# Writing 128 KB of zeros through the store queue at the start of a row normalisation

## The chip, the core and the metric

The kernel runs on one core of a Trainium2 chip. A core has several engines that run their own instruction streams: VectorE (DVE in the profile), ScalarE (ACT), GpSimd (POOL), TensorE (PE, idle here) and SyncE (SP). Data move between the device's memory (HBM) and the on-chip memory (SBUF, 128 partitions) by DMA: an instruction on SP's or ACT's queue issues a transfer, and 16 DMA engines carry it out. The metric is device time in microseconds (us) of one execution, as the median of several runs. A profile is one further execution with a recorder on; its times belong to that execution.

## What is computed

Each row of 1024 numbers is divided by the sum of its absolute values.

```python
batch, seq, dim = 32, 512, 1024        # x: float32
def reference(x):
    sums = np.sum(np.abs(x), axis=-1, keepdims=True)
    return (x / (sums + 1e-8)).astype(np.float32)
```

That is 16,384 rows of 4 KB: 67.11 MB are read and 67.11 MB written.

## The kernel before

The rows are cut into 11 tiles. A tile holds `k` rows in each of the 128 partitions: `k` is 12 for the first ten tiles and 8 for the last (`rows`, L34). Tiles 0, 1 and the last (tile 10) come from the first 4096 rows of `x`, where a partition owns 32 neighbouring rows; tiles 2 to 9 are blocks of 1536 rows each (`piece`, L36). Tile 9 is the block that ends with the last row of the matrix, so the store of tile 9 is the one that writes the last 32 rows. In every tile a partition's rows are contiguous in HBM, so one DMA packet carries 48 KB (32 KB in the last tile), and a transfer has 128 such packets, eight on each DMA engine.

For each tile, in order:

- L88: SP issues the load into `x_tile`, one of four buffers (`BUFS`, L30). The first four loads need no buffer to come free. Load i+4 waits until the store of tile i has left the same buffer.
- L52 to L61: VectorE sums absolute values along the rows (`tensor_reduce`), adds the small constant and takes the reciprocal.
- L63, L70, L73: the rows are scaled in place, most of them by VectorE in one instruction with a broadcast factor (L63), a few one by one on VectorE (L70) or on ScalarE (L73), as `split` (L83) says for the first three and the last two tiles.
- L91: ACT issues the store of the tile.

The order is written out by hand (`manual_schedule`, L85): instructions stand on each engine in program order. SP's queue holds loads alone (the DMA queue q1), and ACT's queue holds stores alone (q10) among its scalings. Both queues are served by the same 16 DMA engines.

Of the kernel before, what the change touches and what calls it, by code (L numbers as in the profile page):

```python
# [1 line left out]

# [4 lines left out]

FP32 = mybir.dt.float32
EPS = 1e-8


@with_exitstack
def kernel(
    ctx: ExitStack,
    tc: tile.TileContext,
    x: bass.AP,
    out: bass.AP,
):
    nc = tc.nc
    P = nc.NUM_PARTITIONS  # L20

    x_flat = x.flatten_outer_dims()
    out_flat = out.flatten_outer_dims()
    n, d = x_flat.shape

    R = 12
    BUFS = 4  # L30
    HEAD = 32
    per_partition = n // P
    assert n % P == 0 and (per_partition - HEAD) % R == 0
    rows = [R] * ((per_partition - HEAD) // R + 2) + [HEAD - 2 * R]  # L34

    def piece(flat, i):  # L36
        head = flat[: P * HEAD, :].rearrange("(p r) d -> p r d", p=P)
        if i < 2:
            return head[:, R * i : R * (i + 1), :]
        if i == len(rows) - 1:  # L40
            return head[:, 2 * R :, :]
        a = P * (HEAD + R * (i - 2))
        return flat[a : a + P * R, :].rearrange("(p r) d -> p r d", p=P)

    sbuf = ctx.enter_context(tc.tile_pool(name="sbuf", bufs=BUFS))
    stats = ctx.enter_context(tc.tile_pool(name="stats", bufs=len(rows)))

    def normalize(x_tile, k, kv, kt):


        s = stats.tile([P, R], FP32)
        nc.vector.tensor_reduce(  # L52
            out=s[:, :k],
            in_=x_tile[:, :k, :],
            axis=mybir.AxisListType.X,
            op=mybir.AluOpType.add,
            apply_absolute_value=True,
        )
        nc.vector.tensor_scalar_add(out=s[:, :k], in0=s[:, :k], scalar1=EPS)  # L59
        inv = stats.tile([P, R], FP32)  # L60
        nc.vector.reciprocal(out=inv[:, :k], in_=s[:, :k])  # L61
        if kv:
            nc.vector.tensor_mul(  # L63
                out=x_tile[:, :kv, :],
                in0=x_tile[:, :kv, :],
                in1=inv[:, :kv].unsqueeze(2).to_broadcast([P, kv, d]),
            )
        for r in range(kv, kv + kt):
            row = x_tile[:, r, :]
            nc.vector.tensor_scalar_mul(out=row, in0=row, scalar1=inv[:, r : r + 1])  # L70
        for r in range(kv + kt, k):
            row = x_tile[:, r, :]
            nc.scalar.activation(  # L73
                out=row,
                in_=row,
                func=mybir.ActivationFunctionType.Copy,
                scale=inv[:, r : r + 1],
            )

    last = len(rows) - 1
    split = {0: (3, 4), 1: (0, 3), 2: (0, 3), last - 1: (0, 2), last: (5, 3)}  # L83

    with tc.manual_schedule():  # L85
        for i, k in enumerate(rows):
            x_tile = sbuf.tile([P, R, d], FP32)
            nc.sync.dma_start(out=x_tile[:, :k, :], in_=piece(x_flat, i))  # L88
            kt, ks = split.get(i, (0, 0))
            normalize(x_tile, k, k - kt - ks, kt)  # L90
            nc.scalar.dma_start(out=piece(out_flat, i), in_=x_tile[:, :k, :])  # L91


# [1 line left out]
_INS = ['x']  # L95
_OUTS = [((32, 512, 1024), 'float32')]


# [23 lines left out]
```

## Time and profile before

| | before |
|---|---|
| median of 3 runs | 317.42 us (317.39 to 317.75) |
| span of the profiled execution | 315.8 us |
| VectorE busy | 261.2 us, 83% of the span |
| ScalarE busy | 17.4 us, 6% |
| mean rate of the DMA engines | 425 GB/s over the span |
| loads: issue to landing, median of the ten of 6 MB | 38.0 us |
| stores: issue to landing, median of the ten of 6 MB | 47.4 us |
| first load issued / first tile's reduction begins | 0.73 / 17.65 us |
| first store issued | 38.67 us |
| last store issued | 294.08 us |

The span is the time from the first to the last instruction in the profile. The time of a run is somewhat larger, since it holds what lies around these instructions. Engines overlap, so busy shares do not add up; what counts is which wait ends last. The "chain of waits" follows the work back from the last instruction to whatever released it. A table of stretches gives, for windows of the span, how long each engine was busy and how much the DMA engines moved (a packet is counted where it starts). The packet records of the trace give start, length, size and queue of each DMA packet; the records of one DMA engine can be strung together, because each packet starts where the one before it ended.

### The profile page before, as it was taken

What the parts mean: (1) busy time and instruction counts of PE and PEld (TensorE: products, weight loads), DVE (VectorE), ACT (ScalarE), POOL (GpSimd) and SP (SyncE); (2) the same over time, 40 slices, a digit from 0 to 9 for tenths busy, and PEclk for the clock granted to TensorE, in tenths of its full rate; (3) what the DMA queues carried; (4) which work ended last, traced back from release to release, by engine and by line L of the source; (5) the groups of instructions that cost most, each with busy time, mean ns of one, the idle gap of its engine ahead of it and who ended that gap; (6) DMA issues with size and microseconds to landing.
All of it is one profiled execution on the core that took longest, in us unless ns stands there. A gap on an engine that the chain in (4) does not pass through costs nothing.

```text
span 315.8 us, 168 instructions
## 1 busy us (share of the span) xinstructions
DVE 261.2 (83%) x51; ACT 17.4 (6%) x16; POOL 0.2 (0%) x4
## 2 busy tenths in 40 slices
DVE  0079999999999999969996999799699969999200
ACT  0010404004000000000000000000000000201200
POOL 0000000000000000000000000000000000000000
DMA  8999999999999999999999999999999999999986
GB/s 324 473 398 448 448 361 430 405 486 405 405 486 405 405 486 411 423 467 405 448 436 411 479 405 411 473 417 405 473 417 411 467 413 450 421 442 423 473 374 282
DMA packets 3168, 134.22 MB, mean 425 GB/s; under 512 B 352, under 2 KB 352, under 8 KB 352
## 3 DMA queue, kind: packets, MB, share of 16 engines
q1 hardware_dynamic: 1584, 67.11, 49.8%
q10 hardware_dynamic: 1584, 67.11, 49.1%
HBM read 67.11 MB, written 67.11 MB: 425 GB/s over the span
## 4 chain that ended last, share of the span: by engine, by line
DVE 41%; DMA 33%; another core or an unknown queue 18%; issue 0%; SPq 0%; DVEq 0%
DVE s L52 23%; DMA x_tile<-in_x_dram 17%; DMA out_dram<-x_tile 16%; DVE x_tile L63 15%; DVE x_tile L70 1%; DVE inv L61 0%; DVE s L59 0%; SPq L88 0%; DVEq L117 0%
## 5 line engine op out<-in xcount | busy, mean ns | idle before, releaser
L52 DVE TENSOR_REDUCE s<-x_tile 128x12 f32<-128x12288 f32 (+1 forms) x11 | 138.2, 12561 | 31.5 <-DMA x_tile<-in_x_dram 31.5
L63 DVE TENSOR_TENSOR x_tile<-x_tile,inv 128x12288 f32<-128x12288 f32 (+3 forms) x10 | 113.6, 11358 | 0.5
L73 ACT ACTIVATE x_tile<-x_tile,inv 128x1024 f32<-128x1024 f32 x15 | 16.1, 1138 | 258.7 <-DVE inv L61 258.7
L70 DVE TENSOR_SCALAR x_tile<-x_tile,inv 128x1024 f32<-128x1024 f32 x8 | 5.5, 748 | 0.0
L61 DVE RECIPROCAL inv<-s 128x12 f32<-128x12 f32 (+1 forms) x11 | 2.5, 226 | 0.4
L73 ACT ACT_TABLE_LOAD x1 | 1.3, 1283 | 17.7 <-DMA x_tile<-in_x_dram 17.7
L59 DVE TENSOR_SCALAR s<-s 128x12 f32<-128x12 f32 (+1 forms) x11 | 1.9, 173 | 0.4
L106 POOL MEMSET const-bfloat16-1.0<- 128x1 bf16 x1 | 0.1, 102 | 0.0
L106 POOL MEMSET const-uint8-127<- 128x1 uint8 x1 | 0.1, 102 | 0.0
L106 POOL MEMSET const-float32-0.0<- 128x1 f32 x1 | 0.1, 99 | 0.2 <-issue 0.2
L106 POOL MEMSET const-float32-1.0<- 128x1 f32 x1 | 0.1, 99 | 0.0
## 6 DMA issues: line engine op xcount, KB each, us to landing
x_tile<-in_x_dram SPq DMA_DIRECT2D x10, 6144.0 KB, 38.0
out_dram<-x_tile ACTq DMA_DIRECT2D x10, 6144.0 KB, 47.4
x_tile<-in_x_dram SPq DMA_DIRECT2D x1, 4096.0 KB, 33.3
out_dram<-x_tile ACTq DMA_DIRECT2D x1, 4096.0 KB, 20.6
```

The costliest lines, as they stand in the source:

```text
L52: nc.vector.tensor_reduce(out=s[:, :k], in_=x_tile[:, :k, :], axis=mybir.AxisListType.X, op=mybir.AluOpType.add, apply_absolute_value=True,)
L59: nc.vector.tensor_scalar_add(out=s[:, :k], in0=s[:, :k], scalar1=EPS)
L61: nc.vector.reciprocal(out=inv[:, :k], in_=s[:, :k])
L63: nc.vector.tensor_mul(out=x_tile[:, :kv, :], in0=x_tile[:, :kv, :], in1=inv[:, :kv].unsqueeze(2).to_broadcast([P, kv, d]),)
L70: nc.vector.tensor_scalar_mul(out=row, in0=row, scalar1=inv[:, r : r + 1])
L73: nc.scalar.activation(out=row, in_=row, func=mybir.ActivationFunctionType.Copy, scale=inv[:, r : r + 1],)
L106: nc = _bacc.Bacc("TRN2", target_bir_lowering=False, num_devices=1)
```

## The change

Before the first load, VectorE fills a small tile of 16 partitions by 2 rows by 1024 floats with zeros, and ACT issues a store of it to the last 32 rows of the result: 128 KB in one contiguous piece, with 8 KB from each of the 16 partitions. The store of tile 9 later writes the same rows. The loop's body is split into three functions, and the first four loads stand ahead of the loop; the order of loads on SP, of stores on ACT and of the computation on VectorE is the same.

```diff
+    tiles = {}
+
+    def load(i):
+        x_tile = tiles[i] = sbuf.tile([P, R, d], FP32, name="x_tile")
+        nc.sync.dma_start(out=x_tile[:, : rows[i], :], in_=piece(x_flat, i))
+
+    def store(i):
+        nc.scalar.dma_start(out=piece(out_flat, i), in_=tiles[i][:, : rows[i], :])
+
+    def compute(i):
+        k = rows[i]
+        kt, ks = split.get(i, (0, 0))
+        normalize(tiles[i], k, k - kt - ks, kt)
+
     with tc.manual_schedule():
-        for i, k in enumerate(rows):
-            x_tile = sbuf.tile([P, R, d], FP32)
-            nc.sync.dma_start(out=x_tile[:, :k, :], in_=piece(x_flat, i))
-            kt, ks = split.get(i, (0, 0))
-            normalize(x_tile, k, k - kt - ks, kt)
-            nc.scalar.dma_start(out=piece(out_flat, i), in_=x_tile[:, :k, :])
+        zero = ctx.enter_context(tc.tile_pool(name="zero", bufs=1)).tile([16, 2, d], FP32, name="zero")
+        nc.vector.memset(zero, 0.0)
+        late = out_flat[n - 32 :, :].rearrange("(p r) d -> p r d", p=16)
+        nc.scalar.dma_start(out=late, in_=zero)
+        for i in range(BUFS):
+            load(i)
+        for i in range(len(rows)):
+            compute(i)
+            store(i)
+            if i + BUFS < len(rows):
+                load(i + BUFS)
```

## The prediction

> **What bounds the kernel now.** I read the table of DMA queues first, since the kernel only divides rows and moves every byte twice.
>
> ```profile
> ## 3 DMA queue, kind: packets, MB, share of 16 engines
> q1 hardware_dynamic: 1584, 67.11, 49.8%
> q10 hardware_dynamic: 1584, 67.11, 49.1%
> HBM read 67.11 MB, written 67.11 MB: 425 GB/s over the span
> ```
>
> q1 carries SP's loads, q10 ACT's stores. Their packets fill 98.9% of the 16 DMA engines' time: the transfers bound the kernel, and about 3.5 us of the span (1.1% of 315.8) is theirs to lose. Next, the chain of waits.
>
> ```profile
> 0.73 16.89 DMA x_tile<-in_x_dram
> 17.62 0.02 issue
> 17.65 12.96 DVE s L52
> ...
> 219.13 38.10 DMA x_tile<-in_x_dram
> 257.23 0.02 issue
> 257.25 12.96 DVE s L52
> ```
>
> VectorE waits 17.65 us for tile 0, and later some 2.5 to 2.9 us a tile for loads. It is not the bound at the end either: the last store is issued at 294.08 us, when, by the packet records, the engines still have some 9 us of the store before it to write (that one's last packets end at 303.3 to 304.7). So VectorE may be a few us late without an effect, and the end is set by how soon each DMA engine gets through its bytes. Third, the table of stretches: where do the engines fall short?
>
> ```profile
> core 0: us, DVE busy (x) ACT busy (x) POOL busy (x), PEclk, DMA share, GB/s
> 8.00:38.60 30.60, 20.85 (x8) 5.55 (x5) 0.00 (x0) 1.00 0.99 429
> 40.60:43.60 3.00, 3.00 (x1) 0.00 (x0) 0.00 (x0) 1.00 0.92 262
> 70.00:280.00 210.00, 195.15 (x32) 5.41 (x5) 0.00 (x0) 1.00 1.00 434
> 280.00:313.00 33.00, 13.90 (x9) 3.23 (x3) 0.00 (x0) 1.00 0.97 422
> ```
>
> Between 70 and 280 us they move 434 GB/s, which is 27.1 GB/s each, so 48 KB in 1.81 us. The stretch from 40.6 stands out. ACT issues the first store of all at 38.67, and this is the first moment at which q10 has anything to move. The DMA view in slices of 0.2 us counts each packet where it starts; the first line is for 30 to 38 us, the second for 38 to 46, the third for 0 to 8.
>
> ```profile
> GB/s 0 0 0 0 0 0 737 2212 983 0 0 0 0 0 0 492 2212 1229 0 0 0 0 0 0 492 1475 1966 0 0 0 0 0 0 492 1229 1966 246 0 0 0
> GB/s 0 0 492 1229 1966 246 0 0 0 0 0 0 983 2703 246 0 0 0 0 0 0 0 0 0 0 0 0 983 2458 246 0 0 246 0 0 0 983 2212 492 0
> GB/s 0 0 0 0 0 0 0 0 1475 1966 246 246 0 0 0 0 0 0 0 0 492 2212 1229 0 0 0 0 0 0 492 1475 1966 0 0 0 0 0 0 492 1229
> ```
>
> The 16 engines start packets in near step, a burst every nine slices, or 1.8 us (first line). In the second line the bursts at 40.4 to 41.0 and 43.4 to 44.0 lie three us apart: every engine spends 2.9 to 3.1 us on the load packet ahead of its first store packet, a **pause** of about 1.2 us (one engine, by its packet records, loses 2.3). In the third line the first packets take 2.4 us in place of 1.8: an excess of 0.62 at the start. Together this closes the account of an engine: packets from 1.75, plus 134.22 MB / 16 / 27.1 GB/s = 309.5, plus 0.62, plus 1.2, makes 313.1; twelve engines end at 313.0 to 313.3. The other four end at 314.0 to 314.4: the one with the long pause, and three that lose a few tenths when stores complete. The last store lands at 314.7 and the span ends at 315.8. The median of the runs, 317.42, is 1.62 more; I keep that offset, and changes are counted in the span.
>
> **The change, part by part.**
> *The reordered calls.* Loads stay on SP in the same order, four ahead, then each behind the same store; stores and VectorE's instructions too. Removed: nothing. Cost 0, with nothing needed to hide it.
>
> *The memset* of 16x2048 f32 on VectorE is in no row of before. Below it is bounded by the POOL memset of 128x1, 0.10 us; above by the rate of L63 (12958 ns for 12288 elements, so 2048 in 2.2 us). I take twice the L70 row (748 ns for 1024 elements, one f32 input): 1.5 us. VectorE idles until 17.65, which hides it; without that cover the 1.5 us would fall on an engine with some 9 us of slack at the end, so still nothing.
>
> *ACT's issue and its wait.* ACT waits for the memset, then issues (0.34 to 0.38 us as its other stores). Behind it on ACT stands the table load at 17.70 and the first scaling at 31.10, which wait longer anyway. If VectorE may begin when SP does (0.73), the issue is at about 0.73 + 1.5 + 0.1 = 2.3. From issue to the first packets SP's first load took 1.0 us, and the first store some 1.9, so the zeros reach the engines at about 3.3 to 4.2, while these are in the first load packets (1.7 to 4.4) or just behind them; with the bounds of the memset, 1.9 to 4.9.
>
> *The overwriting store* (tile 9, issued at 281.61), or even all stores if each waited for the zeros, would wait for something over by 10 us; the first store is at 38.67. Cost 0.
>
> *The bytes.* 8 KB on each engine at 27.1 GB/s is 0.30 us, and it is on the path, since no engine idles between 2 and 313 us. Bounds: 0.30, and as much as a pause (1.2) if 16 neighbouring partitions feed 16 engines worse than 128 do, which no row shows. I take 0.30.
>
> *The pause.* This decides, and no row settles it, because in the trace q10 turns from empty to busy just once (from 38.67 on, each store is issued before the one ahead has landed). Two readings fit. Either it belongs to the very first use of q10, and then the zeros take it over from the first store; or it belongs to every turn from empty to busy, and then both pay it, as q10 lies empty from some 5 to 38.67. The zeros' own pause lies between 0 (inside the excess of the first load packets) and 1.2 (the row at 40.6, nearest in queue and direction). As the zeros arrive while the 0.62 of the start runs or has just run, I take 1.2 - 0.62 = 0.6. What goes at 40.6 lies between 0 and 1.2; I take 0, the return of the pause: in the trace it goes with a queue that was empty, and nothing marks it as once for all.
>
> The Trainium skill, "DMA: Bandwidth & Descriptors", section "Queues, rings and completion order", says that an engine takes the queues that have work in turn, changing over at packet ends, and names no price for a queue that comes to life. By it the zeros would cost their 0.30 us alone; the row at 40.6 shows 1.2 us lost at just such a moment, so I go by the row. The same page's section "Rules for kernel authors" speaks against the change: under 64 KB a transfer is mostly overhead, and its fit for GpSimd's queue (about 2 us plus bytes by 436 GB/s) would make 2.3 us of these 128 KB, an estimate; but the page puts most of the 2 us down to the completion, for which nothing here waits.
>
> **Sum.** 0.30 + 0.6 + 0 = +0.9 us: span 316.7, time 318.3, or 0.28% more. With the bounds of the zeros' pause alone this case runs from 317.7 to 318.9.
>
> **Rivals.**
> *Moved, not hidden (not slower by more than can be told).* The pause belongs to the first use; the first store loses its 1.2, the zeros pay 0.6 to 1.2. Total 0.30 + (0.6 to 1.2) - 1.2 = -0.3 to +0.3: 317.1 to 317.7, at the upper end 317.7. For it: q10's later stores show no pause. Against: their queue was never empty.
> *Paid early and hidden (faster).* First use, and at the start it costs next to nothing, since the engines are waiting for their first bytes or because 8 KB behave otherwise than 48: 0.30 - 1.2 = -0.9: 316.5; if the engine with 2.3 us and the late three gain too, 316.2. For it: the 0.62 in which the first packets run idle. Against: the zeros must be there before about 3 us, and by my working they come at 3.3. It decides from the point at which the zeros' pause is under 0.3 us.
> *Two full pauses.* 0.30 + 1.2 = 318.9; with unequal feeding 319.3. For it: the loads are at full rate from 4.4 on, as they were at 40.
> *It does not spread.* If the piece went through one engine, 128 KB / 27.1 GB/s = 4.8 us would fall on it, and the end would move with it: 322. Against: 16 outer rows in the pattern, while the 128-row transfers are spread evenly.
>
> **How the numbers follow.** Forecast (pause returns, partly overlapped) 0.32; two full pauses 0.11; moved 0.29; hidden 0.27; not spread 0.01. Time 318.3, that of the likeliest. The range is 316.3 to 319.0, as hidden and two pauses are too likely to leave out; the likeliest one's own is 317.7 to 318.9. A measurement of this kernel tells about 0.2% (0.63 us) from no change: faster means under 316.8, slower over 318.05. Faster: hidden, and a little of moved: 0.31. Slower: two pauses, the forecast without its lowest part, not spread: 0.41. The rest 0.28.
>
> **What would show it.** Profile after: a burst of packets at 40.4 still followed by one three us later, and an early gap between bursts over 1.8 us beyond the first, confirm the forecast. Bursts 1.8 us apart around 40 mean first use; then the early gaps tell moved from hidden. The zeros' issue should stand at about 2.3, q10 at 1616 packets (16 of data, 16 of completion more), and the first tile should land 0.9 us later than 17.62. The forecast is wrong if the pause is gone at the first store.

## The result, and the profile after

The changed kernel takes 318.01 us (median of 19 runs, 317.49 to 318.39) against 317.37 us for the kernel before (19 runs, 316.66 to 319.12). The ratio is 1.0021, with a 95% interval of 1.0013 to 1.0028: slower by 0.64 us, or by 0.4 to 0.9. The profiled execution has a span of 316.2 us in place of 315.8. The forecast was 318.3. Ratios, here and below, leave out the three runs (two with 48 KB zeros, one with a 24 KB first store) that were over 1.5% above the fastest of their kernel; medians hold them.

The page after shows the added work, in its tables of queues, of instruction groups and of DMA issues:

```profile
q1 hardware_dynamic: 1584, 67.11, 49.6%
q10 hardware_dynamic: 1616, 67.24, 49.1%
HBM read 67.11 MB, written 67.24 MB: 425 GB/s over the span
...
L96 DVE MEMSET zero<- 16x2048 f32 x1 | 1.8, 1765 | 1.2 <-PEq L120 1.2
...
out_dram<-zero ACTq DMA_DIRECT2D x1, 128.0 KB, 7.6
```

The store queue has 32 packets more, 16 of data and 16 that signal completion. The timeline of the first 20 us of the changed kernel (start, length, engine and instruction, and in brackets the idle time before and what ended it) shows when they were issued:

```profile
0.73 1.89 SPq L82 DMA_DIRECT2D x_tile<-in_x_dram  x4
1.21 1.76 DVE L96 MEMSET zero<- 16x2048 f32 x1 [1.21 <-PEq L120]
3.01 0.38 ACTq L98 DMA_DIRECT2D out_dram<-zero  x1
17.94 12.95 DVE L47 TENSOR_REDUCE s<-x_tile 128x12 f32<-128x12288 f32 x1 [14.96 <-DMA x_tile<-in_x_dram]
```

The first tile's reduction starts at 17.94, which is 0.29 later than before (17.65). Now the DMA view of the changed kernel in slices of 0.2 us, first for 4 to 12 us and then for 38 to 46 us:

```profile
GB/s 246 1475 1966 246 0 0 0 0 0 246 1229 2212 246 0 0 0 0 0 41 164 860 2048 1475 0 0 0 0 0 0 492 1720 1720 0 0 0 0 0 0 492 1475
```
```profile
GB/s 0 0 0 0 492 1720 1720 0 0 0 0 0 0 492 1475 1966 0 0 0 0 0 0 0 0 0 246 0 246 1229 1475 492 246 0 0 0 0 246 983 1475 492
```

In the first line the zeros start where the small numbers stand (41 and 164 GB/s, from 7.6 us), and the next load packets follow 0.3 us behind them. Bursts of load packets lie nine slices apart before that and ten to eleven across it: 1.81 us of a load packet and 0.31 us of zeros, with **no pause**. In the second line the first store still has its pause: bursts at 40.8 to 41.2 and mostly at 43.6 to 44.2, about three us apart. So the pause neither moved to the zeros nor was paid twice.

The table of stretches after, with the same windows as before:

```profile
8.00:38.60 30.60, 20.55 (x7) 5.55 (x5) 0.00 (x0) 1.00 1.02 440
40.60:43.60 3.00, 3.00 (x1) 0.00 (x0) 0.00 (x0) 1.00 1.06 295
70.00:280.00 210.00, 196.01 (x32) 5.41 (x5) 0.00 (x0) 1.00 1.00 433
280.00:313.00 33.00, 13.34 (x9) 3.23 (x3) 0.00 (x0) 1.00 0.99 429
```

The steady rate is the same (433 against 434 GB/s) and the stretch at 40.6 is still the lowest; a packet counts where it starts, so windows shifted by 0.3 us against the packets differ by some per cent.

Strung together by DMA engine, the packet records give the end of each engine's last packet. The middle of the sixteen moves from 313.22 to 313.39 us, and the slowest from 314.39 to 314.44. In both kernels a few engines end about 1 us behind the others, and the slowest of them sets the span. After, these are two that took one load packet more ahead of the first store packet and lost 2.0 us there in place of 0.8 to 1.3. On fifteen engines of the kernel before this loss is 1.1 to 1.3 us, a little more, so the middle moves by less than the 0.30 us of the bytes.

### The profile page after: what moved, and what is told of

It reads as the page before. It is cut to its first block, busy times and chain, and to the rows that moved or that the text cites. A ratio compares the mean times of both kernels' runs of the same rounds, so it can differ in the third digit from the quotient of the medians.

```text
span 316.2 us, 170 instructions
## 1 busy us (share of the span) xinstructions
DVE 263.0 (83%) x52; ACT 17.4 (6%) x16; POOL 0.2 (0%) x4
## 4 chain that ended last, share of the span: by engine, by line
DVE 41%; DMA 33%; another core or an unknown queue 18%; issue 0%; SPq 0%; DVEq 0%
DVE s L47 23%; DMA x_tile<-in_x_dram 17%; DMA out_dram<-x_tile 16%; DVE x_tile L58 15%; DVE x_tile L65 1%; DVE inv L56 0%; DVE s L54 0%; SPq L82 0%; DVEq L131 0%
## 5 line engine op out<-in xcount | busy, mean ns | idle before, releaser
L96 DVE MEMSET zero<- 16x2048 f32 x1 | 1.8, 1765 | 1.2 <-PEq L120 1.2
```

The lines of the kernel that those rows point to most:

```text
L96: nc.vector.memset(zero, 0.0)
```

## The experiments

Each run was compared with the kernel before on the same chip. Medians of before beside these runs were 317.2 to 317.4 us. An interval of some 0.12 to 0.2% on either side is usual here, since the runs of before alone spread over 316.5 to 319.3; on single packets the records of the profiles say more than the medians. All edits are against the changed kernel unless something else is said.

**The calls without the zeros, and 8 KB of zeros in place of 128.**

```diff
-        zero = ctx.enter_context(tc.tile_pool(name="zero", bufs=1)).tile([16, 2, d], FP32, name="zero")
-        nc.vector.memset(zero, 0.0)
-        late = out_flat[n - 32 :, :].rearrange("(p r) d -> p r d", p=16)
-        nc.scalar.dma_start(out=late, in_=zero)
```

> The zeros and their store are left out; the split into functions and the loads ahead of the loop stay. Theory A (the zeros cost their bytes, 0.30 us, and something of about 0.3 us that comes with an extra transfer at the front): as before, 317.4, ratio 1.000. Theory B (the reordered calls cost the part that the bytes do not explain): 317.7, ratio 1.001. First store's pause near 40 us as before.

Measured: 317.38 us, ratio 0.9991 (0.9976 to 1.0007). The reordered calls cost nothing that can be told. In its profile the first store has its pause (0.9 to 1.3 us), seven engines take one load packet more ahead of it, and nine of the sixteen end at 313.9 to 314.2 us: engines fall behind without any zeros too.

```diff
-        zero = ctx.enter_context(tc.tile_pool(name="zero", bufs=1)).tile([16, 2, d], FP32, name="zero")
+        zero = ctx.enter_context(tc.tile_pool(name="zero", bufs=1)).tile([16, 128], FP32, name="zero")
-        late = out_flat[n - 32 :, :].rearrange("(p r) d -> p r d", p=16)
+        late = out_flat[n - 2 :, :].rearrange("r (q c) -> (r q) c", c=128)
```

> The zeros shrink to 16 x 512 B (8 KB in all, 0.02 us of each DMA engine). Bytes alone: 317.4, ratio 1.000. A fixed price of an extra transfer at the front: 317.7, ratio 1.001. The pause at the first store stays about 1.2 us if a small transfer does not take it over, and goes if first use of the queue were the cause (after's trace says that it stays).

Measured: 317.59 us, ratio 1.0009 (0.9991 to 1.0028), which decides nothing between 317.4 and 317.7. The records say more: each engine slips its 512 B in between two load packets at about 6 us, in 0.03 us, and the loads go on at 1.81 us each. The first store has its pause of 0.6 to 1.2 us, and on seven engines a second one of 0.2 to 0.4.

**Larger zeros.** First one packet of 48 KB for each engine, out of the fourth buffer ahead of its load:

```diff
-        for i in range(BUFS):
+        for i in range(BUFS - 1):
             load(i)
+        spare = tiles[BUFS - 1] = sbuf.tile([P, R, d], FP32, name="x_tile")
+        nc.vector.memset(spare[:16, :, :], 0.0)
+        late = out_flat[n - 16 * R :, :].rearrange("(p r) d -> p r d", p=16)
+        nc.scalar.dma_start(out=late, in_=spare[:16, :, :])
+        nc.sync.dma_start(out=spare[:, : rows[BUFS - 1], :], in_=piece(x_flat, BUFS - 1))
```

> Zeros of 16 x 48 KB, one packet of 48 KB for each DMA engine, out of the fourth buffer, which is loaded after that (its load is issued at about 20 us in place of 2, and still long before its turn). Bytes: 1.81 us on each engine, so 319.2, ratio 1.006. If the pause belongs to large packets, the zeros pay one too (a load packet of some 3 us just ahead of them): 320.4, ratio 1.0095; and if it is paid once only by large packets, the first store has none: 319.2 with a clean stretch at 40 us.

Measured: 326.02 us, ratio 1.0237 (1.0197 to 1.0277), far above every expectation, and for another reason. The engines' packets of zeros lasted from 1.8 to 7.8 us, where a store packet of 48 KB out of 128 partitions takes 1.81. So sixteen engines that read 48 KB each from 16 neighbouring partitions were slow and uneven here, and the engines did not get into step again. (The profile is of the slowest run, 329.35 us; the fastest took 323.23, still far above before.) The load packets just ahead of the zeros lost between nothing and 0.9 us, too mixed to settle the question about packet size, which stays open in this run.

Then 1 MB out of all 128 partitions, eight packets of 8 KB for each engine:

```diff
-        zero = ctx.enter_context(tc.tile_pool(name="zero", bufs=1)).tile([16, 2, d], FP32, name="zero")
+        zero = ctx.enter_context(tc.tile_pool(name="zero", bufs=1)).tile([P, 2, d], FP32, name="zero")
-        late = out_flat[n - 32 :, :].rearrange("(p r) d -> p r d", p=16)
+        late = out_flat[n - 2 * P :, :].rearrange("(p r) d -> p r d", p=P)
```

> Zeros of 128 x 8 KB (1 MB), eight small packets for each DMA engine. Bytes: 64 KB by 27.1 GB/s = 2.42 us, so 319.8, ratio 1.0076. If the pause belongs to several packets that arrive at once on an empty queue, the zeros pay it: 321.0, ratio 1.0114, with a load packet of some 3 us just ahead of them. If it belongs to packet size, no pause at the zeros and the usual one at the first store.

Measured: 320.95 us, ratio 1.0110 (1.0091 to 1.0128). The number is that of the theory which had a pause at the zeros, and the trace says that this theory is wrong all the same. DMA view from 4 to 12 us:

```profile
GB/s 0 1229 1475 1229 0 0 0 0 0 0 1229 1475 983 246 0 0 0 0 0 205 451 1679 1761 492 0 0 0 0 0 0 246 1065 1556 1475 246 0 0 0 0 0
```

Load packets and packets of zeros take turns (a small figure, then the large burst), each round 2.12 us long, 1.81 + 0.31. All but one engine end between 315.2 and 315.9, some 2.2 us later than before's middle, as 8 x 0.31 = 2.47 us of zeros would have it, less a smaller pause at the first store (0.7 to 0.8). One engine falls behind from 160 us on and ends at 317.6; it makes the rest of the 3.5 us.

**The zeros behind the first four loads on SP's queue.**

```diff
-        nc.scalar.dma_start(out=late, in_=zero)
         for i in range(BUFS):
             load(i)
+        nc.sync.dma_start(out=late, in_=zero)
```

(The memset moves with them.)

> The same 128 KB of zeros, issued by SP behind the first four loads, so that no other queue is busy at the start and the zeros go out behind the loads at some 60 us. Theory A (8 KB cost each engine 0.30 us wherever they stand, and the rest of the 0.64 is a shift of the first store's arrival against the packet ends): 317.7, ratio 1.001, with before's spread. Rival B (the rest comes with any extra transfer): 318.0, ratio 1.002.

Measured: 318.87 us, ratio 1.0056 (1.0038 to 1.0074): both expectations missed. The same 0.31 us of zeros went out at 82 to 84 us, between the fourth load and the fifth. Within the next 10 us, twelve of the sixteen engines had load or store packets longer by 0.13 to 1.4 us each, and the middle engine ends at 314.5. All six runs are slower than the median of before, by 0.9 us at least. That the small packets set off the long ones is not shown: with the reordered calls alone seven engines lost 0.4 to 0.6 us in load packets at 102 us, and the time stayed.

**What the pause at the first store belongs to.** No zeros; the first tile's store goes out in three transfers, so in packets of 16 KB:

```diff
     def store(i):
+        if i == 0:
+            for r in range(0, R, 4):
+                nc.scalar.dma_start(out=piece(out_flat, i)[:, r : r + 4, :], in_=tiles[i][:, r : r + 4, :])
+            return
```

> No zeros; the first tile's store goes out as three transfers of four rows, in packets of 16 KB (0.60 us) in place of 48 KB (1.81 us). Theory A (the pause comes from the size of the store queue's first packets: an engine reads a whole store packet ahead of the load data that it owes, 1.81 less some 0.6 that it is ahead anyway): no pause at 40 us; it comes back, if at all, when the 48 KB packets of the second store begin beside loads. Rival B (it belongs to the first large stream of stores, whatever its packets): 1.0 to 1.3 us at 40 us as before. Time within 0.5 us of before either way, 317.4.

Measured: 316.49 us, ratio 0.9983 (0.9966 to 1.0000). Stretches of this run, and its DMA view from 38 to 46 us:

```profile
8.00:38.60 30.60, 20.71 (x7) 5.55 (x5) 0.00 (x0) 1.00 0.98 426
40.60:43.60 3.00, 3.00 (x1) 0.00 (x0) 0.00 (x0) 1.00 1.02 437
```
```profile
GB/s 0 0 246 1475 1475 737 0 0 0 0 0 0 0 819 410 82 2458 1229 246 0 0 0 0 0 0 737 410 164 1966 1475 492 0 0 0 0 0 0 573 573 164
```

The dip at 40.6 us is gone: 437 GB/s where the kernel before has 262. Store packets (the small bursts at 40.6, 43.0 and 45.4) and load packets take turns in rounds of 2.4 us, 1.81 + 0.61, with 0.1 to 0.3 us lost at the first. A second loss of some 0.6 us follows in the load packet at 46.2. All engines end between 312.65 and 313.28, and no one is left behind.

This run shows a second thing. Its load queue is empty from about 69.3 us, when the fourth load has landed, until the next load is issued at 76.66. The DMA view from 74 to 82 us, where the last four bursts are at 75.6 to 76.4, 77.6, 79.4 and 81.2:

```profile
GB/s 573 328 328 655 246 328 737 246 819 1966 737 492 0 0 0 0 0 246 2212 983 492 0 0 0 0 0 0 2212 1229 492 0 0 0 0 0 0 2212 1229 492 0
...
q10 hardware_dynamic: 107, 3.06, 88.7%
q1 hardware_dynamic: 16, 0.79, 22.7%
```

The burst at 81.2 is the first of the returning loads (q1's 16 packets), beside stores that are running, and the bursts stay 1.81 us apart (in the packet records no 48 KB packet takes longer than 1.82 us from there until 129 us): a queue that turns from empty to busy, with packets of 48 KB, and **no pause**.

With two transfers, so in packets of 24 KB (`range(0, R, 6)`):

> No zeros; the first tile's store in two transfers of six rows, packets of 24 KB (0.91 us). Theory A (pause = the packet's time less about 0.6): some 0.3 us at the first store packet, and 316.5 to 316.8 if no engine falls behind. Rival B (a pause of fixed size once packets are over some size): 1.2 us at the first store packet, and 317.2 to 317.4.

Measured: 317.82 us, ratio 1.0010 (0.9992 to 1.0029). Fourteen engines lose 0.3 to 0.7 us at the first store packet and 0.2 to 0.3 a round later; two lose 1.0. Two engines end at 315.4 to 315.5 while the middle engine ends at 312.76. So on most engines the first loss is smaller than with 48 KB, though more than expected (0.3), and in the profile two engines that fall behind set the end.

**The moment of the first store.** No zeros; the scaling of the first tile is split otherwise, `split = {0: (5, 4), ...}` for an earlier store (37.98 us) and `{0: (0, 4), ...}` for a later one (39.93).

> No zeros; tile 0 scales two more rows one by one on VectorE, so its store is issued about 0.9 us earlier, half a packet. Theory A (before's runs spread over 316.4 to 318.3 because the first store's arrival falls just on the packet ends, so that some engines take one more load first and lose about 1 us more): all engines take the same order, and the runs gather at the low end, 316.5, ratio 0.997. Rival B (the moment of arrival is of no account): as before, 317.4 with the same spread.

> No zeros; tile 0 scales its rows in VectorE's one broadcast instruction, so its store is issued about 1.1 us later, a little over half a packet. Theory A: as in the run with the earlier store, all engines in one order and 316.5, ratio 0.997. Rival B: as before, 317.4.

Measured: 317.40 us, ratio 1.0015 (1.0001 to 1.0028), with the earlier store; 317.92 us, ratio 1.0023 (1.0012 to 1.0035), with the later one. My theory of the spread fell in both. With the earlier store all engines took the same order, as it had it, but one still ended at 314.03 against 313.15 for the middle one, and no run was under 317.1. With the later store six engines took one more load first, and these and one other ended between 313.7 and 314.6. So one order for all is not enough to keep every engine in step. That the later store makes the kernel slower is not shown by its spans (315.58 us on average, before 315.53): most of the difference lies outside the span, as worked out below.

**The zeros together with the small first store, and both kernels once more.**

> The change's zeros together with the first tile's store in three transfers of 16 KB packets, to be set against the run with these three transfers alone on the same chip, which spreads little. Theory A (the zeros cost 0.30 us of bytes on every engine, and the further 0.3 us of the change was engines that fell behind at the first store): 0.3 us more than that run, with as small a spread. Rival B (the zeros bring a further fixed loss of about 0.3 us, whatever follows): 0.6 us more.

> The kernel with the first tile's store in three transfers of 16 KB packets and no zeros, once more, on the chip of this call: 316.5, ratio 0.997 to 0.998 against before, runs within 0.3 us of each other but for strays.

Measured on one chip: with the zeros 316.96 us, ratio 0.9996 (0.9983 to 1.0009), nine of eleven runs within 316.77 to 317.15; without them 317.20 us, ratio 0.9993 (0.9974 to 1.0012), runs from 316.35 to 319.18. The small first store's own gain did not come back, as one engine fell behind in the profiled execution, most of it at 272 us (it ends at 314.31, the middle one at 312.95), so it can't be called faster than before. By the medians the zeros cost nothing in this pair; by the lowest run they cost 0.4 us (316.77 against 316.35), by the middle engine's end 0.2 to 0.3 (313.11 against 312.95, and 312.83 in the earlier run). So it doesn't decide between the two expectations, 0.3 and 0.6. And the changed kernel with a small first store is about 1 us under the changed kernel as it is (316.96, ratio 0.9996, against 318.0, ratios 1.0021 and 1.0032), with the same zeros, on other chips.

> The changed kernel once more, for a second profile and a second set of runs. Theory A (every engine gets 0.30 us of bytes; what comes on top depends on which engines fall behind in a run): the sixteen engines' usual end again some 0.25 to 0.3 us later than before's, one or more engines about 1 us behind them, runs from some 316.8 up, median 317.6 to 318.0. Rival B (a further fixed loss on every engine): the usual end 0.6 us later than before's, and no run under 317.4.

Measured: 317.99 us, ratio 1.0032 (1.0015 to 1.0050), runs from 317.65. The middle engine ends at 313.54, 0.32 later than before's, as theory A had it; the slowest ends at 314.40, span 316.0. But no run came in under 317.65, as rival B had it: neither is decided.

The ends of the engines in these profiles, in us from the span's start (worked out from the packet records):

```
                                middle   slowest   span
before                          313.22   314.39    315.8
reordered calls alone           313.95   314.18    315.7
changed                         313.39   314.44    316.2
changed, once more              313.54   314.40    316.0
512 B packets of zeros          313.30   314.15    315.7
earlier first store             313.15   314.03    315.4
later first store               313.22   314.63    315.9
small first store               312.83   313.28    314.8
small first store, once more    312.95   314.31    315.8
24 KB first store               312.76   315.54    317.1
zeros and small first store     313.11   313.75    315.0
eight times the zeros           315.43   317.60    319.2
zeros on SP's queue             314.50   315.84    317.4
```

The span follows the slowest engine, 1.3 to 1.8 us behind it. Two profiles can differ by more than the zeros' bytes for other reasons: with the reordered calls alone, without zeros, the middle engine ends later than in either profile of the change.

## Why the prediction held, and where it did not

**The bytes.** The term of 0.30 us is what the traces show: one packet of 0.31 us on each engine, and the first tile later by 0.29.

**The time at which the zeros arrive** was wrong. They were issued at 3.01 in place of 2.3 (the memset began at 1.21, not 0.73, and took 1.77, not 1.5), and the first packet started at 7.7 in place of 3.3 to 4.2. From issue to first packet took 4.7 us; I had taken 1.0 from a load on idle engines and 1.9 from the packet that carries the first store's pause. The first store's own packets, in the same row of before, came 4.8 us after its issue, and that was the row to take.

**The pause at the zeros**, the step "As the zeros arrive while the 0.62 of the start runs or has just run, I take 1.2 - 0.62 = 0.6", failed: it measured 0 in both profiles of the change, and 0 with 512 B and ahead of the first of eight packets of 8 KB. The sign named for it, a first tile that lands 0.9 us later, failed with it (0.29). The reading behind it, a pause at every turn from empty to busy, failed too, in the run whose load queue ran empty and came back without one.

**The pause at the first store stays** was right, in both profiles of the change, but not for the reason given. The first-use reading would have had it go, and the rivals "moved" and "hidden" rest on it; all fell. What the runs show is a loss at the first store packet of 1.1 to 1.3 us for 48 KB on fifteen engines of before, 0.3 to 0.7 for 24 KB on fourteen engines, at most 0.5 for 16 KB in three profiles, and nothing for the zeros of 8 KB and 512 B. But size alone does not order it: behind the 1 MB of zeros 48 KB lost 0.7 to 0.8, and with the losses that follow within a few us 24 KB and 16 KB come to the same 0.6 to 1.0. An engine that reads a whole store packet while it owes the rest of a load, and is about 0.6 us ahead, would give 1.2, 0.3, 0 and 0 us. That is near, but the second losses (0.6 us at 46.2 in the 16 KB run) are not in it; the losses are measured, the mechanism is argued.

The Trainium skill's rule, in "DMA: Bandwidth & Descriptors", section "Queues, rings and completion order", that an engine takes its queues in turn at packet ends, holds for the zeros: their 8 KB and 512 B packets slip in with nothing lost. The sum of 0.30 us by it was the better one for this term, and I had put the row of a 48 KB packet above it for a packet of 8.

**The sum** came out near (0.9 forecast, 0.64 measured, 0.4 to 0.9 by the interval) by luck, with a term of 0.6 in it that is not there. What stands in its place is known in part.

The offset between span and time, which the prediction kept at 1.62 us, did not stay. Time less span is 1.63 us on average for the kernel before (1.58 to 1.70 in the 95 runs beside the experiments) and 1.77 for the change (1.73 to 1.82 in all 28 runs): 0.14 us of the 0.64 lie outside the span. It does not take zeros to move it: the reordered calls alone have 1.64, but the runs without zeros and with another first store have 1.77 to 1.80, and that with the later store 2.19. What sets it no run shows.

With the bytes' 0.30 that makes 0.44. The interval leaves from nothing to 0.45 us over, that of the second set of runs 0.04 to 1.1. The reordered calls do not explain it (ratio 0.9991). A further fixed loss on all engines is not seen in the profiles (middle engine later by 0.17 and 0.32), but single profiles differ by more than that. What differs in the runs is the low end, and the spans show it without the offset: 48 of the 95 runs of before are under 315.7 us, and none of the 28 of the change (on the chip of the second set 7 of 14, and none of 9). In the change's two profiles two and four engines took one load more at the first store and fell behind, and the same zeros with a small first store gave 316.96. That points to engines left behind more often, but **it is not shown**: with the reordered calls alone seven engines took one load more, in a kernel as fast as before, and the slowest engine in the profiles of the change is hardly later than in the one of before (314.44 and 314.40 against 314.39). What the rest is, and why the zeros should bring it about, stays open.

**The rest.** No cost is seen of the reordered calls (ratio 0.9991), of the memset and ACT's wait (the zeros are issued at 3.01 us, and VectorE's first reduction waits for its load until 17.94) or of the overwriting store (issued at 281.04 us, before at 281.61).

## What to carry to other kernels

Where DMA engines are busy from end to end, every byte added takes its time on them, however early it is sent: price it by the steady rate of one engine. Don't price a pause for a small packet by a row of the same queue with packets six times as large. When a change is worth tenths of a us, compare spans as well as times, since what lies outside the span can change by as much. And look at each engine's own end: the span belongs to the slowest of sixteen, which can hide or double an effect of a few tenths of a us.

## What was not expected of the hardware

- A transfer issued beside running 48 KB loads started its first packet 4.7 to 5 us after the issue (zeros of 8 KB: 3.01 to 7.7; of 512 B: 1.01 to 6.0), against 1.0 us for the first load on idle engines.
- Store packets of 48 KB from 16 neighbouring partitions took 1.8 to 7.8 us in one profile, those of 8 KB from 16 partitions 0.31, the steady rate.
- A packet's own cost is small: 0.309 us for 8 KB and 1.815 us for 48 KB put, by a straight line, some 8 ns on each.
- Time less span differs between kernels that do nearly the same: 1.63 us before, 1.77 with the change, 2.19 with the later store.
